# The dense loop's order: whole v rows, v's low parts apart from u's, u's high parts behind the gelu

## The chip, the cores and the metric

The kernel runs on one core of a Trainium2 chip. The metric is the time of one execution on the device, in microseconds (us). The median of three runs of the kernel before is 1834.13 us (1832.16 to 1834.73).

## The reference

One layer on x (512 tokens, 1024 features): a mixer of mLSTM and differential attention, a cross-attention into a fixed memory, and a PEER expert mixer, each behind an RMS norm, and a last norm. The change lies in the PEER part:

```python
def block(xb):
    q = (xb @ w_pq).reshape(PEER_BLOCK, PEER_HEADS, 2, PEER_HALF)
    ...
    eidx = jnp.take_along_axis(cand_i, best_j, axis=-1)
    gate = jax.nn.softmax(best_v, axis=-1)
    u = peer_u[eidx]
    act = jax.nn.gelu(jnp.einsum('td,thkd->thk', xb, u).astype(jnp.float32), approximate=False)
    coef = (gate * act).astype(xb.dtype)
    return jnp.einsum('thk,thkd->td', coef, peer_v[eidx])
```

Each token picks 128 experts (8 heads, 16 each) of 16384. An expert has a row of 1024 in peer_u and one in peer_v.

## The kernel before, in words

The tokens are four blocks of 128. Blocks 0 and 1 are done sparsely: for each of 128 slots a row for every token is gathered from peer_u, VectorE forms the dot product with the token, and later the rows of peer_v are gathered and summed. Blocks 2 and 3 are done densely. There W holds, for every expert and each of the 256 tokens, the gate or zero, and all experts are worked through in 128 groups of 128. The dense loop (lines 1222 to 1239) has one iteration for each group i:

- `load_u` (1151) and `load_v` (1156) bring one group's rows, 512 KB each, by DMAs that SP issues. The raw u tile has two buffers of a whole row, the raw v tile three buffers of half a row.
- Products are taken in three passes, from a high and a low part of each operand (`three`, lines 314 to 316). `split_u` (1161) makes u's parts: ScalarE casts the high part uH (1168), VectorE subtracts for the low part uL (1169), half a row at a time. `split_v` (1172) does so for v, with vH on ScalarE (1177) and vL on POOL (1178).
- `apply_u` (1181) is the first product, 24 matmuls of 256 columns into ua. `gate_u` (1191) takes the gelu on ScalarE (1195), multiplies by W on VectorE (1196) and casts the high part pH on ScalarE (1198). `low_p` (1201) subtracts for pL on VectorE (1204). `apply_v` (1207) is the second product, 12 matmuls of 512 columns, added up in four PSUM tiles acc over all groups. It runs one iteration behind.
- `feed("half")` (1231, 1234) puts the sparse work of block 1 between these, 2.1 items an iteration: a dot or a sum on VectorE (983, 1038) and, on POOL, the gather that refills the tile which it frees (917). This side work is used up some six iterations before the loop's end; `finish` then adds the rows of x2, which it loads, on VectorE (954).

PE, VectorE, ScalarE and POOL take the loop's instructions in the order in which it is written (`manual_schedule`, 1219). SP's queue is put in order by the scheduler; it is first in, first out, so a load that waits for a buffer holds up those behind it.

Of the kernel before, what the change touches and what calls it, by code (L numbers as in the profile page):

```python
# [8 lines left out]
F32 = mybir.dt.float32  # L9
I32 = mybir.dt.int32  # L10
U32 = mybir.dt.uint32
F32R = mybir.dt.float32r
# [7 lines left out]
P = 128  # L20
S = 512
D = 1024
# [11 lines left out]
TD = NDENSE * P  # L34
# [51 lines left out]
def layer_kernel(ctx, tc, x, mem, norm_mix_g, w_in, conv_w, b_igate, b_fgate, ml_norm_g,  # L86
# [8 lines left out]
    nc = tc.nc  # L95
# [3 lines left out]
    vf = peer_v[0]  # L99
# [17 lines left out]
    def ps(name):  # L117
        return psums[0](name)
# [54 lines left out]
    def ft(shape, tag, name, bufs=2, dt=F32):  # L173
        return home[0].tile(shape, dt, tag=tag, name=name, bufs=bufs)

    def mt(shape, tag, name, bufs=2, dt=F32):
        return mp.tile(shape, dt, tag=tag, name=name, bufs=bufs)
# [30 lines left out]
    def w2(name):  # L208
        return mt([P, 512], "w2", name, bufs=5)
# [116 lines left out]
    def low(dst, src, high):  # L326
        kind = LOW[min(lows[0], len(LOW) - 8 + lows[0] % 8)] if group[0] else LOW_FIRST[lows[0] % 8]
        lows[0] += 1
        e = nc.gpsimd if kind == "pool" else nc.vector
        e.tensor_sub(dst, src, high.bitcast(F32))  # L330

    def w_parts(src, c0, name, split):

        for q in range(2):
# [6 lines left out]
            if group[0] or rings["wH"] and lows[0] % 2:  # L341
                H = ft(sh, "wH", f"{name}H{q}", bufs=rings["wH"], dt=F32R)
            else:
                H = keep.tile(sh, F32R, tag="hv", name=f"{name}H{q}", bufs=2)
            L = ft(sh, "wL", f"{name}L{q}", bufs=rings["wL"], dt=F32R)
            nc.scalar.copy(H, raw)
            low(L, raw, H)
            yield range(4 * q, 4 * q + 4), (H, L)

# [71 lines left out]
    def feed(where, n=1):  # L421

        owed[0] += n * PACE[where]
        while owed[0] >= 1 and feeder:
            got = next(feeder[0], -1)
            if got is None:
                owed[0] = 0.0
            elif got == -1:
                feeder.pop(0)
            else:  # L430
                owed[0] -= 1
# [26 lines left out]
    def mixers(T0, NT, hT):  # L458
# [174 lines left out]
        def scores(it, _):  # L633
            tt, h = it
            T = T0 + tt
            L = (T + 1) * P
            pc, rs = [], mt([P, 2], "rs", f"rs{T}{h}", bufs=3)
            for c in range(2):
                sp = ps(f"ds{T}{h}{c}")
                nc.tensor.matmul(sp[:, :L], lhsT=daqT[64 * c:64 * c + 64, h, tt * P:(tt + 1) * P],  # L640
                                 rhs=dakT[64 * c:64 * c + 64, h, :L], start=True, stop=True)
                t = w2(f"dp{T}{h}{c}")
# [485 lines left out]
    dp = ctx.enter_context(tc.tile_pool(name="dense", bufs=1, side="right", reuse_waits="tile"))  # L1128

    def half(tag, name, bufs, dt=F32):  # L1130
        return dp.tile([P, 512], dt, tag=tag, name=name, bufs=bufs)
# [3 lines left out]
    for tt in range(NDENSE):  # L1135
        for q in range(2):
            f = half("uH", f"h3d{tt}{q}", 4)
            nc.sync.dma_start(f, h3_d[NB - NDENSE + tt][:, q * 512:(q + 1) * 512])
            fv = f.rearrange("p (k t) -> p k t", k=4)
            sl = (slice(None), slice(4 * q, 4 * q + 4), slice(tt * P, (tt + 1) * P))  # L1140
# [8 lines left out]
    raw_u, raw_v, uT, vs, pp, uo = {}, {}, {}, {}, {}, {}  # L1149

    def load_u(i):

        raw_u[i] = keep.tile([P, D], F32, tag="hv", name=f"ud{i}", bufs=2)
        nc.sync.dma_start(raw_u[i], peer_ut[i])

    def load_v(i):
        raw_v[i] = [half("vR", f"vd{i}{n}", 3) for n in range(2)]
        for n in range(2):
            nc.sync.dma_start(raw_v[i][n], vf[i * P:(i + 1) * P, n * 512:(n + 1) * 512])

    def split_u(i):
        uT[i] = []
        r = raw_u.pop(i)
        for q in range(2):
            sl = slice(q * 512, (q + 1) * 512)
            H = half("uH", f"uH{i}{q}", 4, F32R)
            L = half("uL", f"uL{i}{q}", 3, F32R)
            nc.scalar.copy(H, r[:, sl])  # L1168
            nc.vector.tensor_sub(L, r[:, sl], H.bitcast(F32))  # L1169
            uT[i].append((H, L))  # L1170

    def split_v(i):
        vs[i] = []
        for n, v in enumerate(raw_v.pop(i)):
            H = half("vH", f"vH{i}{n}", 3, F32R)
            L = half("vL", f"vL{i}{n}", 2, F32R)
            nc.scalar.copy(H, v)  # L1177
            nc.gpsimd.tensor_sub(L, v, H.bitcast(F32))  # L1178
            vs[i].append((H, L))

    def apply_u(i):
        o = uo[i] = pq_.tile([P, 512], F32, tag="ua", name=f"ua{i}", bufs=2)
        for q in range(2):
            H, L = uT[i][q]
            for k in range(4):
                kk = 4 * q + k
                sl = slice(k * P, (k + 1) * P)
                three(o[:, :TD], (H[:, sl], L[:, sl]), (hH[:, kk, :], hL[:, kk, :]), kk == 0, kk == ND - 1)
        del uT[i]

    def gate_u(i):

        o = uo[i]
        a = o[:, TD:2 * TD]
        nc.scalar.activation(a, o[:, :TD], AF.Gelu)
        nc.vector.tensor_mul(a, a, W[:, i, :])  # L1196
        H = dp.tile([P, TD], F32R, tag="pH", name=f"pH{i}", bufs=2)
        nc.scalar.copy(H, a)  # L1198
        pp[i] = H

    def low_p(i):
        H = pp[i]
        L = dp.tile([P, TD], F32R, tag="pL", name=f"pL{i}", bufs=2)
        nc.vector.tensor_sub(L, uo.pop(i)[:, TD:2 * TD], H.bitcast(F32))
        pp[i] = (H, L)

    def apply_v(i):
        H, L = pp.pop(i)
        for n in range(2):
            for tt in range(NDENSE):  # L1210
                sl = slice(tt * P, (tt + 1) * P)
                three(acc[tt][n], (H[:, sl], L[:, sl]), vs[i][n], i == 0, i == P - 1)
        del vs[i]

    in_step[0] = True
    load_u(0)
    load_u(1)
    load_v(0)
    with tc.manual_schedule(engines={mybir.EngineType.PE, mybir.EngineType.DVE, mybir.EngineType.Activation,
                                     mybir.EngineType.Pool}):  # L1220
        split_u(0)
        for i in range(P + 1):
            if i + 2 < P:
                load_u(i + 2)
            if i + 1 < P:
                load_v(i + 1)
            if i < P:
                apply_u(i)
            if i + 1 < P:
                split_u(i + 1)  # L1230
            feed("half")
            if i < P:
                gate_u(i)
            feed("half")
            if i < P:
                low_p(i)
                split_v(i)
            if i >= 1:
                apply_v(i - 1)
    owed[0] = 1e9  # L1240
# [33 lines left out]
```

## Time and profile before

| | us |
|---|---|
| median of three runs | 1834.13 |
| the profiled execution | 1837.62 |
| its span | 1835.8 |
| PE busy | 1574.1 |
| VectorE busy | 1363.0 |
| POOL busy | 996.4 |
| ScalarE busy | 748.4 |

The span is the stretch in which the core's engines ran; the profiled execution's own time is 1.8 us longer. The dense loop takes the last 840 us of it or so. In the views PE is the matrix engine, PEld its weight loads, DVE VectorE, ACT ScalarE, POOL GpSimd and SPq the queue on which SP issues DMAs; L1169 is line 1169 of the kernel. A row of a timeline has its start, its length, the engine and line, the tiles written and read, and in brackets how long the engine had idled before and what it waited for.

### The profile page before, as it was taken

How to read it: one execution, taken by the hardware profiler on the slowest of the kernel's cores; microseconds unless marked ns; L12 is line 12 of the kernel's file. 1: busy time of each engine (PE TensorE's matmuls, PEld its weight loads, DVE VectorE, ACT ScalarE, POOL GpSimd, SP SyncE). 2: the span in 40 equal slices, each digit the busy share in tenths (PEclk: the TensorE clock that was granted, in tenths of full speed). 3: DMA queues.
4: the chain of work that ended last, by engine and by line, in shares of the span. 5: the costliest groups of instructions: out<-in, count | busy, mean ns of one | idle time of the engine just before them, and what ended most of it. 6: DMA issues, size and time to landing. Idle time of an engine off the chain costs nothing.

```text
span 1835.8 us, 27918 instructions
## 1 busy us (share of the span) xinstructions
PE 1574.1 (86%) x9561; PEld 1303.4 (71%) x9561; DVE 1363.0 (74%) x3005; ACT 748.4 (41%) x1729; POOL 996.4 (54%) x834
## 2 busy tenths in 40 slices
PE   7998788866648999895798999999999999989986
PEld 6798778864328666772467777777777777778775
DVE  4354499798994111789898888888888888888874
ACT  3554445223333122223687444444444444444433
POOL 2000004788770144225663777777777778778754
PEclk9999889786558999997899999999999999999997
DMA  7758627898992877527776999999999999999983
GB/s 237 249 184 275 229 70 258 292 304 305 341 313 67 275 255 271 186 93 265 240 256 212 338 333 333 327 331 337 329 330 335 333 336 339 328 328 333 335 309 109
DMA packets 211454, 501.16 MB, mean 273 GB/s; under 512 B 20792, under 2 KB 90480, under 8 KB 210544
## 3 DMA queue, kind: packets, MB, share of 16 engines
q0 software_dynamic: 74304, 270.57, 42.2%
q1 hardware_dynamic: 137008, 228.82, 36.6%
q8 instruction: 75, 1.23, 0.3%
q14 instruction: 67, 0.55, 0.1%
HBM read 490.93 MB, written 8.39 MB: 272 GB/s over the span
## 4 chain that ended last, share of the span: by engine, by line
PE 25%; DVE 23%; DMA 16%; issue 15%; POOL 11%; ACT 7%; POOLq 2%; SPq 1%; DVEq 0%; ACTq 0%
DMA vd<-in_peer_v_dram 9%; POOL vL L1178 6%; DVE u L983 5%; DVE uL L1169 3%; DMA u<-in_peer_u_dram,eidx 3%; ACT vH L1177 3%; POOL u L917 3%; PE cqt_o L322 3%; PE vpe L1015 3%; POOLq L1178 2%; PE pqt_o L322 2%; DVE vaccp L1038 2%; POOL v L917 2%; ACT uH L1168 2%; PE cot_o L322 2%
## 5 line engine op out<-in xcount | busy, mean ns | idle before, releaser
L917 POOL DMA_INDIRECT u<-in_peer_u_dram,eidx x256 | 332.4, 1299 | 225.5 <-issue 104.9
L1169 DVE TENSOR_TENSOR uL<-ud,uH 128x512 fp32r<-128x512 f32 x256 | 309.6, 1246 | 117.3 <-ACT uH L1168 113.4
L1178 POOL TENSOR_TENSOR vL<-vd,vH 128x512 fp32r<-128x512 f32 x256 | 350.5, 1386 | 55.0 <-ACT vH L1177 36.4
L314 PE MATMUL ua<-hH,uH 128*128 128x256 f32 x1024 | 290.4, 284 | 3.1 <-ACT hH L1141 3.1
L315 PE MATMUL ua<-hL,uH 128*128 128x256 f32 x1024 | 290.9, 284 | 0.4 <-DVE hL L1142 0.4
L316 PE MATMUL ua<-hH,uL 128*128 128x256 f32 x1024 | 290.8, 284 | 0.0
L315 PE MATMUL acc<-vL,pH 128*128 128x512 f32 x512 | 223.0, 436 | 54.1 <-POOL vL L1178 51.6
L917 POOL DMA_INDIRECT v<-in_peer_v_dram,eidxT x128 | 145.7, 1138 | 196.2 <-PE vpe L1015 164.4
L1198 ACT CAST pH<-ua 128x256 fp32r<-128x256 f32 x128 | 47.7, 372 | 403.1 <-DVE ua L1196 403.1
L314 PE MATMUL acc<-vH,pH 128*128 128x512 f32 x512 | 202.0, 395 | 9.3 <-ACT vH L1177 9.3
L314 PEld LDWEIGHTS ua<-hH,uH 128*128 128x128 f32 x1024 | 196.9, 192 | 8.7 <-ACT hH L1141 3.3
L316 PE MATMUL acc<-vH,pL 128*128 128x512 f32 x512 | 202.5, 396 | 0.0
L315 PEld LDWEIGHTS ua<-hL,uH 128*128 128x128 f32 x1024 | 196.9, 192 | 5.9 <-DVE hL L1142 0.6
L316 PEld LDWEIGHTS ua<-hH,uL 128*128 128x128 f32 x1024 | 197.0, 192 | 0.0
L315 PEld LDWEIGHTS acc<-vL,pH 128*128 128x128 f32 x512 | 96.4, 188 | 133.2 <-POOL vL L1178 119.1
L917 POOL DMA_INDIRECT v<-in_peer_v_dram,eidx x128 | 137.8, 1077 | 75.8 <-DVE vaccp L1038 53.1
L1177 ACT CAST vH<-vd 128x512 fp32r<-128x512 f32 x256 | 154.1, 622 | 47.9 <-DMA vd<-in_peer_v_dram 31.4
L983 DVE SCALAR_TENSOR_TENSOR u<-u,h3k 128x1024 f32<-128x1024 f32 x128 | 154.2, 1218 | 18.7 <-DMA u<-in_peer_u_dram,eidx 17.9
L1038 DVE SCALAR_TENSOR_TENSOR vaccp<-v,gate,vaccp 128x1024 f32<-128x1024 f32 x127 | 162.1, 1277 | 0.2
L983 DVE SCALAR_TENSOR_TENSOR u<-u,h3p 128x1024 f32<-128x1024 f32 x128 | 154.1, 1207 | 0.0
L1168 ACT CAST uH<-ud 128x512 fp32r<-128x512 f32 x256 | 145.7, 616 | 0.7 <-DVE hL L1142 0.7
L314 PEld LDWEIGHTS acc<-vH,pH 128*128 128x128 f32 x512 | 97.3, 190 | 26.4 <-ACT vH L1177 9.5
(636 smaller groups left out, 3200.9 us busy)
## 6 DMA issues: line engine op xcount, KB each, us to landing
ud<-in_peer_ut_dram SPq DMA_DIRECT2D x128, 512.0 KB
vd<-in_peer_v_dram SPq DMA_DIRECT2D x256, 256.0 KB
qkg_w<-in_w_in_dram SPq DMA_DIRECT2D x16, 512.0 KB
dag_w<-in_w_in_dram SPq DMA_DIRECT2D x16, 512.0 KB
wog_w<-in_w_out_dram SPq DMA_DIRECT2D x16, 512.0 KB
vg_w<-in_w_in_dram SPq DMA_DIRECT2D x8, 512.0 KB
og_w<-in_w_in_dram SPq DMA_DIRECT2D x8, 512.0 KB
dvg_w<-in_w_in_dram SPq DMA_DIRECT2D x8, 512.0 KB
```

Of the source, the lines that this page charges most:

```text
L314: nc.tensor.matmul(o, lhsT=l[0], rhs=r[0], start=start, stop=False)
L315: nc.tensor.matmul(o, lhsT=l[0], rhs=r[1], start=False, stop=False)
L316: nc.tensor.matmul(o, lhsT=l[1], rhs=r[0], start=False, stop=stop)
L322: nc.tensor.matmul(o, lhsT=l, rhs=r, start=start, stop=stop)
L917: g = nc.gpsimd.indirect_dma_start(out=u, out_offset=None, in_=src, in_offset=bass.IndirectOffsetOnAxis(ap=eidx[:, s:s + 1], axis=0))
L983: nc.vector.scalar_tensor_tensor(u, u, 1.0, h3, op0=OP.mult, op1=OP.mult, accum_out=act[:, s:s + 1])
L1015: m = nc.tensor.matmul(acc[n][32 * j:32 * j + 32, :], lhsT=zs[0][:, j, c0 + 31 - g:c0 + 63 - g], rhs=fours[g][j][:, n * 512:(n + 1) * 512] ...
L1038: nc.vector.scalar_tensor_tensor(acc, v, c, acc, op0=OP.mult, op1=OP.add)
L1168: nc.scalar.copy(H, r[:, sl])
L1169: nc.vector.tensor_sub(L, r[:, sl], H.bitcast(F32))
L1177: nc.scalar.copy(H, v)
L1178: nc.gpsimd.tensor_sub(L, v, H.bitcast(F32))
```

## The change

- v is loaded a whole row at a time, into two buffers of a row; rows 0 and 1 are loaded ahead of the loop.
- `split_u` becomes `high_u` and `low_u`. The high part of group i+2 is cast right behind the gelu of group i; the low part stays where it was.
- `split_v` becomes `high_v` and `low_v`. Both high parts of v are cast behind uH and ahead of the multiplication by W and of pH. The low part of v's first half is written ahead of the second feed, that of the second half behind it.
- vH has four buffers and not three, vL three and not two, pL one and not two.

```diff
@@ -1154,29 +1154,39 @@
         nc.sync.dma_start(raw_u[i], peer_ut[i])
 
     def load_v(i):
-        raw_v[i] = [half("vR", f"vd{i}{n}", 3) for n in range(2)]
+        t = dp.tile([P, D], F32, tag="vR", name=f"vd{i}", bufs=2)
+        nc.sync.dma_start(t, vf[i * P:(i + 1) * P, :])
+        raw_v[i] = [t[:, n * 512:(n + 1) * 512] for n in range(2)]
+
+    def high_u(i):
+        uT[i] = []
+        for q in range(2):
+            H = half("uH", f"uH{i}{q}", 4, F32R)
+            nc.scalar.copy(H, raw_u[i][:, q * 512:(q + 1) * 512])
+            uT[i].append(H)
+
+    def low_u(i):
+        r = raw_u.pop(i)
+        for q, H in enumerate(uT[i]):
+            L = half("uL", f"uL{i}{q}", 3, F32R)
+            nc.vector.tensor_sub(L, r[:, q * 512:(q + 1) * 512], H.bitcast(F32))
+            uT[i][q] = (H, L)
+
+    def high_v(i):
+        vs[i] = []
         for n in range(2):
-            nc.sync.dma_start(raw_v[i][n], vf[i * P:(i + 1) * P, n * 512:(n + 1) * 512])
-
-    def split_u(i):
-        uT[i] = []
-        r = raw_u.pop(i)
-        for q in range(2):
-            sl = slice(q * 512, (q + 1) * 512)
-            H = half("uH", f"uH{i}{q}", 4, F32R)
-            L = half("uL", f"uL{i}{q}", 3, F32R)
-            nc.scalar.copy(H, r[:, sl])
-            nc.vector.tensor_sub(L, r[:, sl], H.bitcast(F32))
-            uT[i].append((H, L))
-
-    def split_v(i):
-        vs[i] = []
-        for n, v in enumerate(raw_v.pop(i)):
-            H = half("vH", f"vH{i}{n}", 3, F32R)
-            L = half("vL", f"vL{i}{n}", 2, F32R)
-            nc.scalar.copy(H, v)
-            nc.gpsimd.tensor_sub(L, v, H.bitcast(F32))
-            vs[i].append((H, L))
+            H = half("vH", f"vH{i}{n}", 4, F32R)
+            nc.scalar.copy(H, raw_v[i][n])
+            vs[i].append(H)
+
+    def low_v(i, n):
+
+        H = vs[i][n]
+        L = half("vL", f"vL{i}{n}", 3, F32R)
+        nc.gpsimd.tensor_sub(L, raw_v[i][n], H.bitcast(F32))
+        vs[i][n] = (H, L)
+        if n:
+            del raw_v[i]
 
     def apply_u(i):
         o = uo[i] = pq_.tile([P, 512], F32, tag="ua", name=f"ua{i}", bufs=2)
@@ -1193,6 +1203,9 @@
         o = uo[i]
         a = o[:, TD:2 * TD]
         nc.scalar.activation(a, o[:, :TD], AF.Gelu)
+        if i + 2 < P:
+            high_u(i + 2)
+        high_v(i)
         nc.vector.tensor_mul(a, a, W[:, i, :])
         H = dp.tile([P, TD], F32R, tag="pH", name=f"pH{i}", bufs=2)
         nc.scalar.copy(H, a)
@@ -1200,7 +1213,7 @@
 
     def low_p(i):
         H = pp[i]
-        L = dp.tile([P, TD], F32R, tag="pL", name=f"pL{i}", bufs=2)
+        L = dp.tile([P, TD], F32R, tag="pL", name=f"pL{i}", bufs=1)
         nc.vector.tensor_sub(L, uo.pop(i)[:, TD:2 * TD], H.bitcast(F32))
         pp[i] = (H, L)
 
@@ -1216,25 +1229,29 @@
     load_u(0)
     load_u(1)
     load_v(0)
+    load_v(1)
     with tc.manual_schedule(engines={mybir.EngineType.PE, mybir.EngineType.DVE, mybir.EngineType.Activation,
                                      mybir.EngineType.Pool}):
-        split_u(0)
+        high_u(0)
+        low_u(0)
+        high_u(1)
         for i in range(P + 1):
             if i + 2 < P:
                 load_u(i + 2)
-            if i + 1 < P:
+            if 1 <= i and i + 1 < P:
                 load_v(i + 1)
             if i < P:
                 apply_u(i)
             if i + 1 < P:
-                split_u(i + 1)
+                low_u(i + 1)
             feed("half")
             if i < P:
                 gate_u(i)
+                low_v(i, 0)
             feed("half")
             if i < P:
                 low_p(i)
-                split_v(i)
+                low_v(i, 1)
             if i >= 1:
                 apply_v(i - 1)
     owed[0] = 1e9
```

On ScalarE, in the middle of the loop, before (ua is the gelu's tile, from which pH is cast; the numbers tell buffers apart):

```order
L1195 ACTIVATE ua_11268<-ua_11268 128x256
L1198 CAST pH_11306<-ua_11268 128x256
L1177 CAST vH_11313<-vd_11193 128x512
L1177 CAST vH_11317<-vd_11194 128x512
L1168 CAST uH_11364<-ud_11262 128x512
L1168 CAST uH_11368<-ud_11262 128x512
L1195 ACTIVATE ua_11339<-ua_11339 128x256
```

and now:

```order
L1205 ACTIVATE ua_11186<-ua_11186 128x256
L1165 CAST uH_11219<-ud_11182 128x512
L1165 CAST uH_11221<-ud_11182 128x512
L1179 CAST vH_11223<-vd_11115 128x512
L1179 CAST vH_11225<-vd_11115 128x512
L1211 CAST pH_11228<-ua_11186 128x256
L1205 ACTIVATE ua_11255<-ua_11255 128x256
```

The two casts uH moved from the end of the iteration, behind vH, to its start, and pH from ahead of vH to behind both.

On POOL, in the middle of the loop, before (u and v with a count are the tiles of the side work's gathers):

```order
L917 DMA v_3_12656<-in_peer_v_dram,eidx_6912 128x1024
L917 DMA v_4_12663<-in_peer_v_dram,eidx_6912 128x1024
L1178 TENSOR_TENSOR vL_12669<-vd_12545,vH_12668 128x512
L1178 TENSOR_TENSOR vL_12673<-vd_12546,vH_12672 128x512
L917 DMA v_5_12730<-in_peer_v_dram,eidx_6912 128x1024
L917 DMA v_6_12737<-in_peer_v_dram,eidx_6912 128x1024
L1178 TENSOR_TENSOR vL_12743<-vd_12619,vH_12742 128x512
L1178 TENSOR_TENSOR vL_12747<-vd_12620,vH_12746 128x512
```

and now:

```order
L917 DMA v_3_12532<-in_peer_v_dram,eidx_6912 128x1024
L1186 TENSOR_TENSOR vL_12547<-vd_12429,vH_12540 128x512
L917 DMA v_4_12549<-in_peer_v_dram,eidx_6912 128x1024
L1186 TENSOR_TENSOR vL_12554<-vd_12429,vH_12542 128x512
L917 DMA v_5_12604<-in_peer_v_dram,eidx_6912 128x1024
L1186 TENSOR_TENSOR vL_12619<-vd_12501,vH_12612 128x512
L917 DMA v_6_12621<-in_peer_v_dram,eidx_6912 128x1024
L1186 TENSOR_TENSOR vL_12626<-vd_12501,vH_12614 128x512
```

The first vL of a group moved from behind the second gather to between the two.

On SP's queue, which issues the loads, before:

```order
L1159 DMA vd_11335<-in_peer_v_dram 128x512
L1154 DMA ud_11404<-in_peer_ut_dram 128x1024
L1159 DMA vd_11336<-in_peer_v_dram 128x512
L1159 DMA vd_11406<-in_peer_v_dram 128x512
L1154 DMA ud_11475<-in_peer_ut_dram 128x1024
L1159 DMA vd_11407<-in_peer_v_dram 128x512
```

and now:

```order
L1158 DMA vd_10974<-in_peer_v_dram 128x1024
L1154 DMA ud_11113<-in_peer_ut_dram 128x1024
L1158 DMA vd_11043<-in_peer_v_dram 128x1024
L1154 DMA ud_11182<-in_peer_ut_dram 128x1024
L1158 DMA vd_11115<-in_peer_v_dram 128x1024
L1154 DMA ud_11251<-in_peer_ut_dram 128x1024
```

Two half rows of v became one load, and v's load stands in turn with u's.

## Rows read from the trace of the kernel before

**Rows 1.** The page: busy us of engines; uL's group: busy us, mean ns.
```profile
PE 1574.1 (86%) x9561; PEld 1303.4 (71%) x9561; DVE 1363.0 (74%) x3005; ACT 748.4 (41%) x1729; POOL 996.4 (54%) x834
...
L1169 DVE TENSOR_TENSOR uL<-ud,uH 128x512 fp32r<-128x512 f32 x256 | 309.6, 1246 | 117.3 <-ACT uH L1168 113.4
```

**Rows 2.** Windows: length; busy us PE, PEld, DVE, ACT, POOL; PEclk; DMA share; GB/s.
```profile
300.00:320.00 20.00, 17.70 (x140) 17.51 (x138) 18.85 (x32) 7.05 (x10) 13.18 (x10) 0.91 1.02 384
440.00:460.00 20.00, 12.95 (x46) 8.83 (x44) 19.54 (x50) 7.89 (x31) 16.17 (x13) 0.75 0.96 355
994.00:1773.00 779.00, 725.80 (x4347) 611.56 (x4346) 670.13 (x866) 337.90 (x728) 598.14 (x492) 1.00 0.95 332
1100.00:1700.00 600.00, 556.57 (x3330) 468.93 (x3329) 514.81 (x660) 257.47 (x555) 459.92 (x379) 1.00 0.95 332
1804.00:1821.00 17.00, 17.00 (x110) 15.50 (x109) 6.77 (x10) 7.44 (x17) 8.54 (x6) 1.00 0.35 111
```

**Rows 3.** Timeline, gelu on ScalarE: first, 122nd, 125th and 126th of 128.
```profile
994.07 0.37 ACT L1195 ACTIVATE ua<-ua 128x256 f32<-128x256 f32 x1 [0.44 <-PE ua L316]
...
1772.81 0.37 ACT L1195 ACTIVATE ua<-ua 128x256 f32<-128x256 f32 x1
...
1804.12 0.37 ACT L1195 ACTIVATE ua<-ua 128x256 f32<-128x256 f32 x1 [3.50 <-PE ua L316]
...
1809.74 0.37 ACT L1195 ACTIVATE ua<-ua 128x256 f32<-128x256 f32 x1 [2.30 <-PE ua L316]
```

**Rows 4.** Waits, 1100 to 1700: us in total, times, longest.
```profile
DVE uL L1169 <- ACT uH L1168: 87.0, 86, 2.3
...
ACT vH L1177 <- DMA vd<-in_peer_v_dram: 27.8, 38, 1.7
```

**Rows 5.** Timeline of VectorE: start, us, instruction, [idle before].
```profile
1217.37 2.02 DVE L1169 TENSOR_TENSOR uL<-ud,uH 128x512 fp32r<-128x512 f32 x2 [1.30 <-ACT uH L1168]
...
1220.44 0.42 DVE L1196 TENSOR_TENSOR ua<-ua,W 128x256 f32<-128x256 f32 x1
...
1221.91 0.41 DVE L1204 TENSOR_TENSOR pL<-ua,pH 128x256 fp32r<-128x256 f32 x1
1222.86 2.60 DVE L1169 TENSOR_TENSOR uL<-ud,uH 128x512 fp32r<-128x512 f32 x2 [0.53 <-ACT uH L1168]
```

**Rows 6.** Timeline of ScalarE over the same iteration.
```profile
1216.19 0.62 ACT L1177 CAST vH<-vd 128x512 fp32r<-128x512 f32 x1 [0.67 <-DMA vd<-in_peer_v_dram]
...
1217.76 0.36 ACT L1195 ACTIVATE ua<-ua 128x256 f32<-128x256 f32 x1
1220.90 0.37 ACT L1198 CAST pH<-ua 128x256 fp32r<-128x256 f32 x1 [2.77 <-DVE ua L1196]
1221.16 1.15 ACT L1177 CAST vH<-vd 128x512 fp32r<-128x512 f32 x2
1222.21 1.14 ACT L1168 CAST uH<-ud 128x512 fp32r<-128x512 f32 x2
...
1228.62 1.14 ACT L1168 CAST uH<-ud 128x512 fp32r<-128x512 f32 x2
```

**Rows 7.** Chain of waits between 1205 and 1220: start, us, what.
```profile
1210.12 5.98 DMA vd<-in_peer_v_dram
```

**Rows 8.** uL and vL, whole run: count, ns min/median/max.
```profile
L1169 DVE TENSOR_TENSOR uL<-ud,uH x256: 676/910/2891, 988.3 to 1814.0; 128x512 fp32r<-128x512 f32 x128
...
L1178 POOL TENSOR_TENSOR vL<-vd,vH x256: 1268/1292/1807, 995.9 to 1824.1; 128x512 fp32r<-128x512 f32 x128
```

**Rows 9.** Waits of SP's queue, 1100 to 1700.
```profile
SPq L1159 <- POOL vL L1178: 414.2, 176, 4.8
```

**Rows 10.** Timeline of SP's queue: issues of v and u loads.
```profile
1210.12 2.20 SPq L1159 DMA_DIRECT2D vd<-in_peer_v_dram  x2
...
1219.41 0.33 SPq L1154 DMA_DIRECT2D ud<-in_peer_ut_dram  x1
```

**Rows 11.** DMA queues, 1100 to 1700: packets, MB, share.
```profile
q1 hardware_dynamic: 40012, 96.99, 45.6%
```

## The prediction

> **What bounds the kernel now.** I read the page's head first, for the busy shares [rows 1]: PE is busy for 86% of it, so no engine is simply full. The change touches only the dense loop, so next I cut that stage out with the view of busy time by stretch [rows 2]. The loop's first gelu starts at 994.07 and its 122nd at 1772.81 [rows 3]; the reader is to see one gelu for each iteration, so 121 iterations take 778.7 us, 6.44 us each. Six more iterations follow after the sparse side work has ended; there gelu follows gelu in 5.62 us and each waits for PE [rows 3], with the granted clock at 1.00 [rows 2]. So 5.62 us is what PE needs for one iteration, and up to 1772.81 the loop spends 0.82 us more than PE asks for.
>
> The waits of the steady middle, 1100 to 1700 [rows 4], tell who sets the pace. VectorE waits 87.0 us there for ScalarE's uH. It is busy for 514.8 us [rows 2]; both together are 601.8, the whole stretch. So VectorE has no other idle time, and never slack: a ring through VectorE and ScalarE is the bound. The two timelines show it in one iteration [rows 5, 6]: uL starts at 1217.37, W is multiplied in at 1220.44, then ScalarE runs pH at 1220.90, the two vH at 1221.16 and the two uH at 1222.21, and the next uL starts at 1222.86. That turn took 5.49 us, with all in time. It lengthens in two ways. First, vH stands ahead of uH on ScalarE, so a late v row delays uH: vH waited for the load of vd at 1216.19 [rows 6], one of 38 such waits in the stretch, 27.8 us in all [rows 4]. The chain of waits shows it as one piece of 5.98 us [rows 7]. Second, uL lasts 676 ns at its shortest, 2891 at its longest [rows 8] and 1246 in the mean [rows 1], as it meets POOL's vL or not.
>
> DMA is the next limit behind that ring: from 994 to 1773 its 16 engines are busy for 0.95 of the time and move 332 GB/s [rows 2].
>
> **The change, part by part.**
>
> *uH ahead of pH and vH.* For each of the 128 iterations the same two casts run, but uH of iteration i+2 now directly behind gelu i. The next uL then finds its uH done. What goes is the ring's wait: 87.0 us in 92.5 iterations (600 us at 6.49), 0.94 us each, so 114 us over 121 iterations if nothing else were late. VectorE's own work, 514.8 over 92.5, is 5.57 us an iteration.
>
> *vH ahead of pH.* vH now runs while W is multiplied in, where ScalarE idled. It costs nothing while that cover lasts: two uH and two vH take 2.28 us, and pH at 1220.90 had idled 2.77 us behind gelu [rows 6]. If the cover goes, pH and pL slip by what is missing.
>
> *vL apart from uL.* The two POOL subtractions now stand one behind each gather, not both behind the second. The first may start earlier by the second dot, which lies between 1220.44 and 1221.91 [rows 5], and a gather. POOL's sum stays: 459.9 us in 600 [rows 2], 4.97 us an iteration. VectorE gains at most 2 x (1246 - 676) ns an iteration, the mean of uL against its shortest [rows 1, 8], and loses at worst a vL that it still meets, about 1.3 us [rows 8]. I count nothing: with its 5.57 us and no wait VectorE is no longer the limit, and the better case makes that surer.
>
> *Whole-row loads, two deep.* SP issues 128 loads of 512 KB in place of 256 of 256 KB; bytes are the same. Their issue time of 0.33 us on SP is hidden, as SP mostly waits for vL (414.2 us of 600, [rows 9]). A row is now freed only when its second half is subtracted. There is one more vH half, one more vL half and one pL fewer. So pL i must now wait until the second product of i-1 has read the only pL. That product is half of PE's columns, some 2.8 of 5.62 us after gelu's operand is ready; before, pL started 1221.91, 4.2 us after the gelu at 1217.76 [rows 5, 6]. It costs nothing.
>
> *Start and end.* v row 1 is loaded earlier, in a stage that is not DMA-bound; nothing. The wait for the x2 rows at the end of the side work is untouched.
>
> *The sum.* The ring's 114 us are not all kept. PE's 5.62 us an iteration would leave 99 (121 x 0.82). DMA leaves less: at a busy share of 0.95 the same bytes at a full share need 778.7 x 0.95 = 739.8 us, a saving of 39; I take a share of 0.995, since loads and gathers now wait for little, and get 743.5 us, **a saving of 35**. So T falls from 6.44 to 6.14 us, and the profiled execution's 1837.6 to 1802.6. The median of the runs shown lies 3.5 us below that execution, so the forecast against it is **1799 us**. The unknown is what 16 busy engines can move in this mix. The bounds: 332/0.95 = 349 GB/s by the loop itself, and 384 GB/s in 300 to 320, at a share of 1.02 [rows 2]; 440 to 460 shows 355 at 0.96, so 370. I take the loop's own value, since it is the same mix, and keep 384 for the range: 778.7 x 332/384 = 673, less than PE's 680, so 99 us saved at the very best, 1735.
>
> The Trainium skill (DMA: Bandwidth & Descriptors, section Bandwidth) puts the HBM limit of one core at about 358 GB/s. By it the stage would need 778.7 x 332/358 = 722 us, a saving of 57. The row with 384 GB/s stands above that limit, so this trace does not bear it out as a ceiling; the sum goes by the loop's own rows.
>
> **The rivals.**
>
> *More bandwidth than the loop shows.* If the 0.95 holds time in which packets merely wait, the limit is nearer to 370 GB/s: 778.7 x 332/370 = 699, 80 us saved, 1754; half of the way, some 1770. For it: the two stretches above. Against it: both have another mix of packets, and neither lasts.
>
> *uH holds up ScalarE (slower).* uH of i+2 now stands ahead of vH, pH and so of pL and the next uL. It needs u row i+2, whose buffer is freed by uL of iteration i and whose load is queued on SP beside a 512 KB v load. From that load's issue to the next issue of the same buffer there are two iterations, which must hold the landing time L and then two uH (1.14), two vH (1.14), pH (0.37), pL (0.41) and two uL (2.02): 5.1 us by [rows 5, 6]. So T is at least (L + 5.1)/2, and at L = 7.8 the gain is gone. Before does not show L. It is bounded by 5.98 us, for a half row issued at 1210.12 and awaited until 1216.1 [rows 7, 10], and by 9.2: the u load issued at 1219.41 [rows 10] was read at 1228.62 without a wait [rows 6]. The first end gives T = 5.54, no limit, the second 7.15: 121 x 0.71 = 86 us slower, 1920. Between them I go by the rate of SP's queue in the stretch, 96.99 MB in 600 us [rows 11], 162 GB/s: a u row behind a whole v row, 1.05 MB, lands in 6.5 us. That is nearer to the first end and gives T = 5.8, below the DMA time, but with little to spare. A landing time of 8.2 would give 6.65, 25 us slower, 1859; of 7.5, T = 6.3 and 1817.
>
> *Nothing changes.* The share is a mean over 16 engines. If the fullest of them has no idle time at 0.95 already, freeing the ring only moves the wait from uH to a load, and the time stays within 3 us of 1834. For it: loads of 256 KB took 6 us. Against it: VectorE never idles for a gather, and turns of 5.49 us do occur.
>
> **How the numbers follow.** DMA full, 1790 to 1812: 0.45. More bandwidth, below 1790: 0.19. uH late but still a gain, 1812 to 1830: 0.12. Nothing changes: 0.09. uH late at a loss: 0.15. Faster by over 0.2% (3.7 us, about what a measurement of this kernel can tell from no change) is 0.45 + 0.19 + 0.12 = 0.76, the same 0.09, slower 0.15. The range is 1766 to 1840: it leaves out some 0.07 of the large savings below and 0.11 of the losses above; the likeliest case alone is 1790 to 1812.
>
> **What would show it.** Right: VectorE's wait for uH is gone; gelu follows gelu in about 6.14 us; the DMA share from the first gelu to the end of the side work is at 0.98 or more with near 350 GB/s; some wait on loads takes over, small and spread. uL is nearer to 0.9 us than 1.26. Wrong upward: ScalarE waiting at uH for the u load, pL waiting for pH, T above 6.3. Wrong downward: T below 6.0 with over 360 GB/s. The same time with a share of 0.95 would say that one DMA engine or a wait not named here sets the pace.

## The result and the profile after

In eight runs beside eight of the kernel before, the change takes 1820.28 us in the median against 1835.33; the ratio of the means is 0.9893 (95% interval 0.9856 to 0.993). That is 1.1%, some 20 us of 1834 (13 to 26; the medians differ by 15), and not the 35 that the prediction forecast. The profiled execution took 1827.32 us, the longest of its eight, with a span of 1825.4.

The page, busy time of the engines and the groups of the parts (busy us, mean ns | idle before, and what ended it):

```profile
PE 1553.2 (85%) x9561; PEld 1304.0 (71%) x9561; DVE 1250.5 (69%) x3005; ACT 759.2 (42%) x1729; POOL 992.4 (54%) x834
...
L1179 ACT CAST vH<-vd 128x512 fp32r<-128x512 f32 x256 | 146.0, 618 | 140.2 <-DMA vd<-in_peer_v_dram 138.9
...
L1217 DVE TENSOR_TENSOR pL<-ua,pH 128x256 fp32r<-128x256 f32 x128 | 54.4, 425 | 216.9 <-ACT pH L1211 195.5
...
L1172 DVE TENSOR_TENSOR uL<-ud,uH 128x512 fp32r<-128x512 f32 x256 | 195.1, 796 | 7.5 <-PE ua L316 6.3
...
L1165 ACT CAST uH<-ud 128x512 fp32r<-128x512 f32 x256 | 145.8, 617 | 72.5 <-DMA ud<-in_peer_ut_dram 70.1
```

Against [rows 1] uL fell from 1246 to 796 ns, and the 113.4 us that it waited for uH are gone. VectorE is busy for 1250.5 us, 112.5 fewer. But pL now waits 195.5 us for pH, and vH 138.9 us for the load of v.

Windows of the loop, from the first gelu to the 122nd and in the steady middle (length; PE, PEld, DVE, ACT, POOL busy; PEclk, DMA share, GB/s):

```profile
992.00:1766.00 774.00, 712.92 (x4346) 616.90 (x4346) 557.99 (x865) 349.23 (x727) 587.79 (x492) 0.99 0.94 334
1100.00:1700.00 600.00, 551.95 (x3358) 477.88 (x3359) 433.08 (x667) 270.55 (x564) 459.28 (x385) 0.99 0.94 337
```

ScalarE's timeline, the gelu (the first, the 122nd, the 126th and the 127th):

```profile
992.40 0.37 ACT L1205 ACTIVATE ua<-ua 128x256 f32<-128x256 f32 x1 [1.10 <-PE ua L316]
...
1766.38 0.37 ACT L1205 ACTIVATE ua<-ua 128x256 f32<-128x256 f32 x1 [1.65 <-PE ua L316]
...
1799.57 0.37 ACT L1205 ACTIVATE ua<-ua 128x256 f32<-128x256 f32 x1 [2.89 <-PE ua L316]
1805.18 0.37 ACT L1205 ACTIVATE ua<-ua 128x256 f32<-128x256 f32 x1 [2.89 <-PE ua L316]
```

121 iterations take 774.0 us, 6.40 each where before took 6.44 [rows 3], and the end without side work still goes by PE, 5.61 us. So of the 10.4 us between the two profiled spans only 4.8 lie in these iterations; 1.7 lie ahead of the first gelu and 4.0 behind the 122nd. Where the other executions of the change gained the rest of the 20 us, no trace shows. In the middle VectorE is busy for 433.1 us instead of 514.8 [rows 2]; PE is busy no longer than before, and DMA moves hardly more. So VectorE was relieved, and something else took over. The waits of the same 600 us (us in total, times, longest):

```profile
DVE pL L1217 <- ACT pH L1211: 146.1, 83, 4.1
ACT vH L1179 <- DMA vd<-in_peer_v_dram: 112.1, 90, 2.9
POOL vL L1186 <- ACT vH L1179: 107.0, 79, 3.4
...
ACT uH L1165 <- DMA ud<-in_peer_ut_dram: 47.9, 51, 2.6
PE acc L315 <- POOL vL L1186: 45.0, 50, 2.3
...
DVE pL L1217 <- PE acc L316: 11.6, 7, 2.6
```

VectorE's idle time rose from 85.2 us (600 - 514.8) to 166.9, and 146.1 of it is pL waiting for pH. pH waits on ScalarE behind vH, and vH waits for its row, in 90 of some 93 iterations. The two timelines show one such turn, first ScalarE, then VectorE's pL:

```profile
1212.89 1.14 ACT L1179 CAST vH<-vd 128x512 fp32r<-128x512 f32 x2 [2.14 <-DMA vd<-in_peer_v_dram]
1213.94 0.37 ACT L1211 CAST pH<-ua 128x256 fp32r<-128x256 f32 x1
1214.96 0.37 ACT L1205 ACTIVATE ua<-ua 128x256 f32<-128x256 f32 x1 [0.65 <-PE ua L316]
1215.95 1.14 ACT L1165 CAST uH<-ud 128x512 fp32r<-128x512 f32 x2 [0.62 <-DMA ud<-in_peer_ut_dram]
1218.01 1.14 ACT L1179 CAST vH<-vd 128x512 fp32r<-128x512 f32 x2 [0.93 <-DMA vd<-in_peer_v_dram]
```

```profile
1214.34 0.42 DVE L1217 TENSOR_TENSOR pL<-ua,pH 128x256 fp32r<-128x256 f32 x1 [3.04 <-ACT pH L1211]
```

Why is v's row late each time? SP's queue shows when the loads are issued, and the chain of waits from 1204 to 1220 what lies between (start, us, what):

```profile
1204.90 0.33 SPq L1158 DMA_DIRECT2D vd<-in_peer_v_dram  x1
1208.60 0.33 SPq L1154 DMA_DIRECT2D ud<-in_peer_ut_dram  x1
1210.06 0.33 SPq L1158 DMA_DIRECT2D vd<-in_peer_v_dram  x1
...
1217.65 0.33 SPq L1158 DMA_DIRECT2D vd<-in_peer_v_dram  x1
1221.32 0.33 SPq L1154 DMA_DIRECT2D ud<-in_peer_ut_dram  x1
1222.82 0.33 SPq L1158 DMA_DIRECT2D vd<-in_peer_v_dram  x1
```

```profile
by line: DMA vd<-in_peer_v_dram 49.5%; POOL vL L1186 23.3%; issue 13.3%; POOL u L917 13.2%; ACT vH L1179 3.9%; POOLq L917 0.4%; POOLq L1186 0.4%; ACTq L1179 0.1%
...
1204.90 7.91 DMA vd<-in_peer_v_dram
...
1212.89 0.63 ACT vH L1179
...
1215.10 1.23 POOL u L917
...
1216.35 1.28 POOL vL L1186
```

A buffer of v is a ring: 7.91 us of landing, the first vH, the first vL (1213.65 to 1214.94), the gather between the two vL, the second vL until 1217.63, and at 1217.65 the same buffer is issued again. The turn is 12.75 us. The other buffer goes from 1210.06 to 1222.82, 12.76 us. With two buffers each turn serves two iterations: 6.38 us an iteration, the measured pace. SP's waits from 1100 to 1700 show that this is the rule and not one picked turn:

```profile
SPq L1158 <- POOL vL L1186: 110.2, 90, 2.4
```

Of the 94 v loads issued in that stretch, 88 have the next load into their buffer within 0.1 us of their second vL's end. In the mean a row is first read 7.79 us after its issue, the second vL ends 4.96 us later, and the whole turn takes 12.83. No engine is full in this; the pace is a landing time plus the work that frees a row, divided by two.

### The profile page after: what moved, and what is told of

It reads as the page before. It is cut to its first block, busy times and chain, and to the rows that moved or that the text cites. A ratio compares the mean times of both kernels' runs of the same rounds, so it can differ in the third digit from the quotient of the medians.

```text
span 1825.4 us, 27537 instructions
## 1 busy us (share of the span) xinstructions
PE 1553.2 (85%) x9561; PEld 1304.0 (71%) x9561; DVE 1250.5 (69%) x3005; ACT 759.2 (42%) x1729; POOL 992.4 (54%) x834
## 4 chain that ended last, share of the span: by engine, by line
PE 28%; DMA 26%; DVE 18%; POOL 12%; issue 9%; ACT 5%; SPq 1%; POOLq 0%; ACTq 0%; DVEq 0%; another core or an unknown queue 0%
DMA vd<-in_peer_v_dram 20%; POOL vL L1186 6%; DVE u L983 4%; POOL u L917 4%; PE cqt_o L322 3%; PE pqt_o L322 2%; POOL v L917 2%; PE vpe L1015 2%; DVE oj L1105 2%; ACT vH L1179 2%; DMA u<-in_peer_u_dram,eidx 2%; PE ua L315 2%; PE cot_o L322 2%; PE ua L316 2%; PE ua L314 2%
## 5 line engine op out<-in xcount | busy, mean ns | idle before, releaser
L1186 POOL TENSOR_TENSOR vL<-vd,vH 128x512 fp32r<-128x512 f32 x256 | 334.3, 1307 | 163.4 <-ACT vH L1179 159.2
L315 PE MATMUL acc<-vL,pH 128*128 128x512 f32 x512 | 214.3, 418 | 59.3 <-POOL vL L1186 57.5
L917 POOL DMA_INDIRECT v<-in_peer_v_dram,eidxT x128 | 154.7, 1209 | 188.3 <-PE vpe L1015 148.3
L1179 ACT CAST vH<-vd 128x512 fp32r<-128x512 f32 x256 | 146.0, 618 | 140.2 <-DMA vd<-in_peer_v_dram 138.9
L1217 DVE TENSOR_TENSOR pL<-ua,pH 128x256 fp32r<-128x256 f32 x128 | 54.4, 425 | 216.9 <-ACT pH L1211 195.5
L1172 DVE TENSOR_TENSOR uL<-ud,uH 128x512 fp32r<-128x512 f32 x256 | 195.1, 796 | 7.5 <-PE ua L316 6.3
L917 POOL DMA_INDIRECT v<-in_peer_v_dram,eidx x128 | 140.7, 1099 | 20.5 <-DVE ua L1209 7.8
L1205 ACT ACTIVATE ua<-ua 128x256 f32<-128x256 f32 x128 | 47.1, 368 | 227.7 <-PE ua L316 211.4
```

Source lines behind the costliest of these rows:

```text
L315: nc.tensor.matmul(o, lhsT=l[0], rhs=r[1], start=False, stop=False)
L917: g = nc.gpsimd.indirect_dma_start(out=u, out_offset=None, in_=src, in_offset=bass.IndirectOffsetOnAxis(ap=eidx[:, s:s + 1], axis=0))
L1172: nc.vector.tensor_sub(L, r[:, q * 512:(q + 1) * 512], H.bitcast(F32))
L1179: nc.scalar.copy(H, raw_v[i][n])
L1186: nc.gpsimd.tensor_sub(L, raw_v[i][n], H.bitcast(F32))
```

## The experiments

Theory A: that ring paces the changed loop. Theory B: DMA is full at a share of 0.94 already, and the loads are late for that. Beside them stand smaller questions: what each part of the change brought, and whether the order of vH and pH matters. T is the mean time from gelu to gelu over the first 121 iterations of the profiled execution, and the medians of these intervals stand behind it; us is the median of the runs, and the ratio that of the means, to the kernel before, run on the same chip.

| kernel | us | ratio, 95% interval | T, median | GB/s, share |
|---|---|---|---|---|
| the change | 1820.28 | 0.9893 (0.9856 to 0.993) | 6.40, 6.24 | 337, 0.94 |
| e1 W in BF16 | 1806.12 | 0.9892 (0.9854 to 0.993) | 6.35, 6.15 | 337, 0.94 |
| e2 three v rows | 1758.28 | 0.9654 (0.9609 to 0.9699) | 5.93, 5.62 | 361, 0.97 |
| e3 half of v's bytes | 1772.7 | 0.9717 (0.9676 to 0.9758) | 6.05, 5.62 | 311, 0.90 |
| e4 uH part alone | 1815.04 | 0.9949 (0.9919 to 0.9979) | 6.41, 5.84 | 333, 0.94 |
| e5 vL as before | 1812.2 | 0.9927 (0.9893 to 0.9961) | 6.36, 6.12 | 336, 0.93 |
| e6 four half rows of v | 1768.28 | 0.9685 (0.9649 to 0.9721) | 6.01, 5.63 | 355, 0.98 |
| e7 pH ahead of vH | 1788.13 | 0.9805 (0.9768 to 0.9841) | 6.16, 5.74 | 348, 0.96 |
| e8 fewer gathers ahead | 1847.13 | 1.0126 (1.0091 to 1.0162) | 6.66, 6.50 | 320, 0.90 |
| e9 e6 and e7 together | 1760.38 | 0.9673 (0.9638 to 0.9708) | 5.91, 5.62 | 362, 0.98 |
| e10 half loads, whole buffer | 1817.18 | 0.9958 (0.9927 to 0.999) | 6.38, 6.19 | 337, 0.94 |
| e11 before, four half rows | 1805.26 | 0.9914 (0.9886 to 0.9941) | 6.28, 6.14 | 341, 0.96 |
| e12 all buffers deeper | 1744.66 | 0.9576 (0.9548 to 0.9604) | 5.81, 5.62 | 366, 0.98 |

The last column is from 1100 to 1700 us.

**e1 and e2: a third row for v.** To make room for a third row, e1 first makes W in BF16 (which rounds the gates) and changes nothing else:

```diff
-    W = wp.tile([P, P, TD], F32, name="W")
+    W = wp.tile([P, P, TD], BF16, name="W")
```

> The changed kernel with W held in bf16 in place of fp32, which frees room on chip for the next runs and rounds the gates. It is the control: both theories expect the time of the changed kernel within 0.5% (about 0.985 to 0.995 of before), since W is read by one instruction an iteration, 0.42 us long, which has slack.

The ratio is that of the change. So e1 can stand for it, and e2 adds the third row and issues each load one iteration earlier:

```diff
-        t = dp.tile([P, D], F32, tag="vR", name=f"vd{i}", bufs=2)
+        t = dp.tile([P, D], F32, tag="vR", name=f"vd{i}", bufs=3)
...
-            if 1 <= i and i + 1 < P:
-                load_v(i + 1)
+            if 1 <= i and i + 2 < P:
+                load_v(i + 2)
```

> As e1, with three whole-row buffers for v in place of two, each row loaded one iteration earlier. Theory A (the ring of v's two buffers: landing time 7 to 8 us, cast, first vL, gather, second vL, 12.75 us for two iterations): the ring gets three iterations, ScalarE's wait for vd (112 us in 1100 to 1700) falls below 20 us, the DMA share rises to 0.98 and the time falls by 20 us or more against e1. Theory B (DMA full at a mean share of 0.94): landing time grows with the rows in flight to some 12 us, the waits move to ud or to gathers, the share stays at 0.94 to 0.95 and the time is that of e1 within 5 us.

The third row takes 2.4% off (0.9654 to 0.9892). The window of e2 from 1100 to 1700:

```profile
1100.00:1700.00 600.00, 580.22 (x3642) 515.90 (x3641) 502.20 (x701) 283.19 (x607) 491.88 (x410) 1.00 0.97 361
```

The wait of vH for vd has left the list, and the same DMA engines now move 361 GB/s. Theory B falls with that: they were not full at 337.

**e3: half of v's bytes, the same buffers.** This kernel leaves out the second half of each v row, so half of the output columns of the dense blocks aren't the reference's.

```diff
-        nc.sync.dma_start(t, vf[i * P:(i + 1) * P, :])
-        raw_v[i] = [t[:, n * 512:(n + 1) * 512] for n in range(2)]
+        nc.sync.dma_start(t[:, :512], vf[i * P:(i + 1) * P, :512])
+        raw_v[i] = [t[:, :512] for n in range(2)]
```

> The changed kernel, but only the first half of each v row is loaded and both halves are made from it: 0.26 MB of 2.15 MB less for an iteration, and wrong values in half of the output columns of the dense blocks. Theory A: a 256 KB load lands sooner by the share that it has in the ring, some 1.5 to 2.5 us, and T falls to 5.6 to 5.8 us, share 0.90 to 0.94. Theory B: bytes set the time, T falls by 12%, from 6.4 to 5.65 us, at an unchanged share. Both: some 75 to 95 us faster than the changed kernel; if the time falls by less than 40 us neither bytes nor landing time is the bound.

It came out 1.8% below the change, some 32 us, less than e2's gain though the loads of u and v together bring a quarter fewer bytes. Bytes can't be the limit, as the share is only 0.90 here; a shorter landing helps the ring as A wants (vH's wait for v falls from 112.1 to 22.5 us), but by less than the 40 us under which the expectation held that neither bytes nor the landing time is the bound. A had forecast 75 us or more, so it missed here by size. The waits that remain are at uH (64.0 us) and at the first vL (75.9). Taken alone this run is no clear verdict; beside e2 it speaks against B.

**e4: of the whole change only uH behind the gelu,** on the kernel before.

```diff
...
         nc.scalar.activation(a, o[:, :TD], AF.Gelu)
+        if i + 2 < P:
+            high_u(i + 2)
```

> The kernel before with one part of the change alone: uH of iteration i+2 cast right behind the gelu of i; v's loads, casts and low parts as before. Theory A: VectorE's wait for uH goes, but pH, vH and vL follow as before, vL still meets uL, and the half-row ring remains: 5 to 20 us faster than before. Theory B: DMA was full before too, so no change within 4 us. A third (uH's wait for its load holds up ScalarE) would make it slower than before.

This part alone brings 0.5%. Its waits from 1100 to 1700:

```profile
ACT vH L1180 <- DMA vd<-in_peer_v_dram: 89.4, 68, 6.2
ACT pH L1203 <- DVE ua L1201: 82.5, 46, 3.7
DVE uL L1172 <- PE ua L316: 44.1, 32, 3.8
```

The wait for uH is gone here too, and again v's load takes its place, with three half rows as with two whole ones. Half of its iterations take 5.84 us or less, but ten last over 10 us.

**e5: both vL behind the second gather again,** on the change.

```diff
                 gate_u(i)
-                low_v(i, 0)
...
+                low_v(i, 0)
                 low_v(i, 1)
```

> The changed kernel with one part undone: both subtractions for vL stand behind the second gather again. Theory A (ring of v's two row buffers): the row is freed later by what the first vL gained, 1 to 1.5 us in a ring of two iterations, so T grows by 0.3 to 0.7 us where the ring binds: 10 to 40 us slower than the changed kernel, about the kernel before or slower. It would also show uL at 1.1 us or more in place of 0.77, since vL meets uL again. Rival C (the gain over before came from uH and the loads alone): the same as the changed kernel within 4 us.

Its window and VectorE's wait, 1100 to 1700:

```profile
1100.00:1700.00 600.00, 558.19 (x3371) 481.53 (x3370) 579.15 (x663) 274.75 (x561) 455.66 (x385) 0.99 0.93 336
```

```profile
DVE pL L1217 <- ACT pH L1211: 20.5, 19, 2.6
```

VectorE's busy time in the 600 us rises from 433.1 to 579.2, so the separation is what shortened uL. The ratio, 0.9927, can't be told from that of the change, and theory A, which expected 10 to 40 us more, missed. But another limit stands behind the same time. 579.2 busy and 20.5 waiting are 599.7 of 600: VectorE sets the pace here. v's ring doesn't: SP never waits for vL in this stretch, and issues each v load 0.4 us behind a u load, 1.55 us in the mean after the row came free. So e5 doesn't show that VectorE's 146 us were idle anyway; it shows two limits that lie close together.

**e6: v in half rows, four half buffers,** the room of two rows, all else as in the change.

```diff
-        t = dp.tile([P, D], F32, tag="vR", name=f"vd{i}", bufs=2)
-        nc.sync.dma_start(t, vf[i * P:(i + 1) * P, :])
-        raw_v[i] = [t[:, n * 512:(n + 1) * 512] for n in range(2)]
+        raw_v[i] = [half("vR", f"vd{i}{n}", 4) for n in range(2)]
+        for n in range(2):
+            nc.sync.dma_start(raw_v[i][n], vf[i * P:(i + 1) * P, n * 512:(n + 1) * 512])
```

> The changed kernel with v loaded in half rows again, into four half buffers (the same room). Theory A: the first half is freed and its load issued one gather and one vL, 2.7 us, earlier, so the ring of that half is shorter: 0 to 20 us faster than the changed kernel. Rival D (whole rows are what pays: 4 KB pieces and half the DMAs): 5 to 25 us slower than the changed kernel, with vH's wait for vd above 150 us in 1100 to 1700.

The same room and the same bytes, and 2.1% less time than the change, some 38 us where A expected 20 at most. Its window and two of its waits, 1100 to 1700:

```profile
1100.00:1700.00 600.00, 573.19 (x3565) 505.62 (x3565) 491.74 (x695) 280.93 (x595) 487.32 (x407) 1.00 0.98 355
```

```profile
ACT uH L1165 <- DMA ud<-in_peer_ut_dram: 100.2, 77, 3.4
...
ACT vH L1179 <- DMA vd<-in_peer_v_dram: 11.2, 22, 1.9
```

vH's wait for v falls from 112.1 to 11.2 us. The first half's buffer comes free a gather and a vL earlier, and SP issues into it 2.77 us, in the mean, before the second vL ends. What is left on ScalarE is the wait for u's row, which still has two whole buffers. So against four half buffers the whole-row load was a loss inside the change, of about twice what the change as a whole gained.

**e10: half loads into the whole-row buffer.** Is it the size of a load, or when its buffer comes free?

```diff
-        nc.sync.dma_start(t, vf[i * P:(i + 1) * P, :])
+        for n in range(2):
+            nc.sync.dma_start(t[:, n * 512:(n + 1) * 512], vf[i * P:(i + 1) * P, n * 512:(n + 1) * 512])
```

> The changed kernel with two DMAs of half a row each into the whole-row buffer: each half lands for itself as with half rows, but the buffer is freed as a whole. It parts what made half rows fast. Theory A1 (freeing: the load of a half may start when that half is subtracted): as the changed kernel, 0.985 to 0.993 of before. Theory A2 (landing: vH of the first half may start when that half has landed): 0.965 to 0.975.

Small loads don't help while the row comes free as one: 0.9958, no better than the change. It is slightly more than was expected of the theory that freeing decides, and far from e6. With the same loads and the same room, how the buffer comes free decides the time, and the size of the load doesn't. Its waits, 1100 to 1700, have moved, though:

```profile
ACT uH L1166 <- DMA ud<-in_peer_ut_dram: 137.7, 77, 4.0
...
ACT vH L1180 <- DMA vd<-in_peer_v_dram: 59.2, 71, 2.1
```

ScalarE waits more for u's row than for v's, and SP waits for vL only 38 times (45.1 us). So here the lost time shows at u's load more than at v's; why u's row is late in this kernel was not followed.

**e7: pH ahead of vH on ScalarE.**

```diff
-        high_v(i)
         nc.vector.tensor_mul(a, a, W[:, i, :])
...
         nc.scalar.copy(H, a)
+        high_v(i)
```

> The changed kernel with pH cast ahead of the two vH again (uH stays behind gelu). It takes away pL's wait for pH (146 us in 1100 to 1700, on VectorE). Theory A: VectorE is off the bound (433 us busy of 600), and vH now waits for the product with W, some 1.5 us later than needed when the row is in time, so no gain: the same within 6 us or slower by up to 20. Rival E (pL behind a late vH delays uL and so u's loads, and that is the bound): 10 us faster or more.

The ratio falls by 0.9 of a per cent against the change, 16 us; the intervals don't touch. Theory A had expected no gain, and rival E, by which a pL behind a late vH delays uL and u's loads, 10 us or more: that came out. Its waits, 1100 to 1700:

```profile
DVE pL L1217 <- PE acc L316: 66.5, 62, 3.1
ACT vH L1179 <- DMA vd<-in_peer_v_dram: 65.4, 74, 1.8
```

pL no longer waits for pH, which had stood behind a cast that waited for a load. In its place pL waits for its single buffer, 66.5 us in place of 11.6; this wait had been covered. v's ring still turns without slack: in 96 of 97 turns the buffer is issued again within 0.1 us of the second vL's end, but a row is first read 7.30 us after its issue in the mean, where the change took 7.79. So the order is a cost beside the ring's; how it shortens the landing isn't shown.

**e8: four gathered tiles ahead in the loop, not six,** to make the loads land sooner.

```diff
-        while to_gather and len(ahead) < (URING if in_step[0] else URING // 2):
+        while to_gather and len(ahead) < (4 if in_step[0] else URING // 2):
```

> The changed kernel with four tiles of gathered rows ahead in the loop in place of six. Theory A, landing time set by what is in flight on the shared DMA engines: up to two gathers of 512 KB fewer stand before a load, the landing time of 7 to 8 us falls by 1 us or more, T by 0.3 us or more: 15 to 40 us faster. Rival F (landing time is not queueing behind gathers): no change within 5 us. If VectorE begins to wait for gathers, over 30 us in 1100 to 1700, the two effects mix and a slower time tells nothing of the landing time.

It is slower, but VectorE now waits for gathers, 57.0 us for rows of v and 51.2 for rows of u, so the run says nothing on the landing time; inconclusive. A v load issued at 1210.56 still took until 1217.67.

**e9: e6 and e7 together.** The edits are those two.

> The changed kernel with both of the helpful undos: v in half rows in four half buffers, and pH ahead of vH. Theory A: the two are different waits (the freeing of v's buffer; pL and so the next uL behind a late vH), so the gains add in part: a ratio of 0.955 to 0.965 to before, T of 5.8 to 5.95 us, with u's load as the wait that is left. If they are one wait, 0.968 to 0.972 as with half rows alone.

0.9673, not told apart from e6 (0.9685), though its T is shorter by 0.1 us. The 0.955 to 0.965 expected of two waits that add up didn't come; with the ring of v loosened, little is left for the order to win. With W in full precision and the room of the change it has the lowest time, 62 us below the kernel before (1760.38 to 1822.44 on the same chip).

**e11: the kernel before with one more half row of v.**

```diff
-        raw_v[i] = [half("vR", f"vd{i}{n}", 3) for n in range(2)]
+        raw_v[i] = [half("vR", f"vd{i}{n}", 4) for n in range(2)]
...
     load_v(0)
+    load_v(1)
...
-            if i + 1 < P:
+            if 1 <= i and i + 1 < P:
                 load_v(i + 1)
```

> The kernel before with one thing more: four half buffers for raw v in place of three, and row 1 loaded ahead of the loop. Theory A: the late vd (27.8 us of waits on ScalarE in 1100 to 1700) goes, and the ring through uL, W, pH, vH and uH stays: 5 to 25 us faster than before, T not below 6.1. If DMA had been the bound of the kernel before: no change within 4 us.

One buffer more does as much as the whole change (0.9914 and 0.9893, with overlapping intervals). The window and the wait of VectorE, 1100 to 1700:

```profile
1100.00:1700.00 600.00, 575.04 (x3419) 479.92 (x3420) 555.08 (x667) 258.49 (x570) 489.95 (x390) 1.00 0.96 341
```

```profile
DVE uL L1169 <- ACT uH L1168: 44.7, 86, 1.7
```

555.1 busy and 44.7 waiting are 599.8 of 600: the ring through VectorE and ScalarE that the prediction read in the kernel before is still the bound here. Only the part of the wait that came from v's late loads is gone, half of the 87.0 us of [rows 4], and some half of what that freed in an iteration went into VectorE's own work: uL is longer here, 1375 ns in the mean against 1246 [rows 1].

**e12: everything deeper.** W in BF16 as in e1, three rows each of u and v, two pL, pH ahead of vH.

```diff
-        raw_u[i] = keep.tile([P, D], F32, tag="hv", name=f"ud{i}", bufs=2)
+        raw_u[i] = dp.tile([P, D], F32, tag="uR", name=f"ud{i}", bufs=3)
...
-        t = dp.tile([P, D], F32, tag="vR", name=f"vd{i}", bufs=2)
+        t = dp.tile([P, D], F32, tag="vR", name=f"vd{i}", bufs=3)
...
-        L = dp.tile([P, TD], F32R, tag="pL", name=f"pL{i}", bufs=1)
+        L = dp.tile([P, TD], F32R, tag="pL", name=f"pL{i}", bufs=2)
...
```

> The changed kernel with room made by W in bf16 (gates rounded, as in e1): three whole-row buffers for v, three for u in a pool of their own, two for pL, and pH ahead of vH. Theory A: with all landing times covered the loop goes to what PE or the DMA engines give: T between 5.6 (PE) and 5.85 us (2.15 MB at 370 GB/s), a ratio of 0.94 to 0.955 to before, PE never waiting long, DMA share 0.97 or more. If the landing time grows with the loads in flight, the ratio stays at 0.96 to 0.97.

0.9576, a little above the range expected, and the fastest of all. Its waits from 1100 to 1680 (the side work ends soon after), and its window:

```profile
ACT ua L1205 <- PE ua L316: 291.8, 100, 4.0
DVE uL L1172 <- PE ua L316: 95.7, 70, 2.1
```

```profile
1100.00:1680.00 580.00, 570.59 (x3592) 507.13 (x3591) 479.23 (x690) 272.78 (x598) 504.60 (x406) 1.00 0.99 370
```

ScalarE and VectorE wait for PE, which is busy for 570.6 of 580 us. In half of its iterations the loop has come to PE's 5.62 us; the mean is 5.81. Whether DMA, at a share of 0.99, holds back the others was not told apart.

## Why the prediction came out as it did

**Right: what bound the kernel before.** The ring uL, W, pH, vH, uH was the bound: e11 shows it once more with busy and wait adding up to the stretch. Moving uH took its wait away, in the change and in e4.

**Right in the number, not in the reason: vL apart shortens uL, and the time doesn't notice.** uL's mean went to 796 ns where "nearer to 0.9 us" was named, and e5 undoes it without a measurable loss. But VectorE was taken to be off the limit with 5.57 us an iteration whether vL stands apart or not. In e5 it has 6.16 us of work in each (579.2 us in 94) and is the limit again, at about the pace that v's ring gives the change.

**Nearly right: start and end.** The last iterations still go by PE in 5.61 us. Nothing was forecast there; in the profiled pair 1.7 us went ahead of the loop's first gelu and 4.0 behind its 122nd, for which no run shows the cause.

**Luck: the time inside the range.** 1820.28 lies between 1766 and 1840, but not by the likeliest case, 1790 to 1812. The signs that were to show it right, a T of 6.14 and a share of 0.98, didn't appear; a T above 6.3 and pL waiting for pH, named as signs of being wrong upward, did.

**Wrong in size: "DMA leaves less", the term of 35 us.** The term was DMA full at a share of 0.995 and 349 GB/s. The change never came near, 0.94 and 337, and the 121 iterations of the profiled execution are 4.8 us shorter, not 35. And what was taken for the limit is none: e2, e6, e9 and e12 move 355 to 370 GB/s at 0.97 to 0.99. The first rival came nearer: a share of 0.95 wasn't the end, and its 370 GB/s were reached (e12). The Trainium skill (Perfetto Trace Analysis, section Roofline) says that a core which runs alone may go beyond the 358 GB/s; these runs agree with 361 to 370.

**Wrong: "A row is now freed only when its second half is subtracted", without a price.** This is the step that failed. The prediction worked out a ring for u's two buffers, (L + 5.1)/2, and none for v's two, which have the same landing time and behind it a vH, two vL on POOL and a gather, 12.75 - 7.91 = 4.84 us. T is then (L + 4.84)/2. With the L of 6.5 that it took, that gives 5.67 us and no limit; with the 7.91 measured it gives 6.38, and T was 6.40. So both were needed, the ring that was left out and a landing time 1.4 us too short. The ring that the prediction did work out doesn't give the pace: ScalarE got the u rows that it waited for 7.23 us after their issue in the mean, and (7.23 + 5.1)/2 is 6.17. The rival "uH holds up ScalarE" had the mechanism for the wrong load: u's row cost ScalarE 47.9 us, v's 112.1. Its milder case, 1812 to 1830, is where the time came out. e2 and e6 show what the missing price is: 2.4% with a third row, 2.1% with rows freed by halves.

**Wrong: vH ahead of pH "costs nothing while that cover lasts".** The cover was there, W's product, but only for a vH that finds its row. The row was late in nearly each iteration, and pL waited 146.1 us for pH. By e7 the order costs some 16 us.

**Nearly right: the single pL "costs nothing".** It showed in 11.6 us of waits, seven times, for example in an iteration of 10.5 us, on VectorE:

```profile
1188.02 0.43 DVE L1217 TENSOR_TENSOR pL<-ua,pH 128x256 fp32r<-128x256 f32 x1 [2.31 <-PE acc L316]
```

With pH early it becomes 66.5 us (e7). What a second pL alone would bring was not tried: only e12 has one.

**Where the expected gain went, then.** In the 600 us, the ring's 87.0 us of waiting and 81.7 us of VectorE's work were freed. 157.7 of these 168.7 us came back as waits at pL, 146.1 for pH and 11.6 for the buffer.

## What to carry to other kernels

Price a buffer by its whole turn: landing time under the loop's own load, plus all that must run until it is free, divided by the iterations that the buffers cover, and do it for every stream that the edit touches. Where the room is given, try more and smaller buffers that come free one by one: here they beat fewer large ones (e6), and small loads into a buffer that is freed as a whole didn't (e10). When an edit is undone and the time stays, look whether another limit has taken its place, as in e5. On an engine that works in order, an instruction that may wait for a load belongs behind those that other engines wait for.

## What the runs showed of the hardware

- A load of 512 KB for which ScalarE waited took 7.82 us from issue to use in the mean for v and 7.23 for u beside the gathers, while the DMA engines' mean share was 0.94; before, one of half that size took 5.98 us [rows 7]. It isn't a fixed figure: in e5, at nearly the same share and rate (0.93, 336 GB/s), the same loads took 6.76 and 5.55 us. Where a load waits in that time stays open; e8 was meant to tell and didn't.
- The mean share of the DMA engines is no measure of what is left: 337 GB/s at 0.94, 311 at 0.90 (e3), and 370 at 0.99 (e12) in the same loop.
- The Trainium skill (DMA: Bandwidth & Descriptors, section Bandwidth) advises batches of 1 MB or more for the better part of the peak. In this loop v in loads of 256 KB (e6) went with 355 GB/s and in loads of 512 KB with 337, and 256 KB into the whole-row buffers (e10) again with 337: how the buffer came free, not the load's size, set the rate.
